# Three 256-column matmuls a block in the feature-major projections of a two-layer decoder trunk, in place of one of 512 and one of 256

## The chip, the core and the metric

The kernel runs on one core of a Trainium2 chip. The core has engines that run side by side, each with its own stream of instructions: TensorE (matmuls, in the profile PE, with its weight loads apart as PEld), VectorE (DVE), ScalarE (ACT) and GpSimd (POOL); SyncE (SP) starts most transfers here. They meet through semaphores. A matmul takes a stationary operand of 128 x 128, which a weight load brings into the array, and streams the columns of a moving operand past it; the sums go to PSUM, a memory of eight banks of 512 fp32 columns on 128 partitions. The metric is the device time of one execution, in microseconds (us).

## The reference

Two layers of a decoder trunk over 256 tokens of width 2048, in fp32. In both a normed input goes through a mixer and then through a gated MLP of hidden width 5632, each with a residual:

```python
for l in range(DEPTH):
    h = rms_norm(x, mix_norm[l])
    if l % 2 == 0:
        h = mixer_ab(h, ...)   # gMLP and HGRN2, one input and one output projection
    else:
        h = mixer_c(h, ...)    # attention with forgetting, 16 heads, output gate
    x = x + h
    h = rms_norm(x, ffn_norm[l])
    x = x + conv_ffn(h, ffn_w_up[l], ffn_conv_w[l], ffn_conv_b[l], ffn_w_down[l])
```

The gated MLP projects up to 2 x 5632 features, convolves each over three tokens, multiplies `silu(a) * b`, and projects down. Nearly all the arithmetic is in products of a 256 x 2048 (or 256 x 5632) activation with weights that are used once.

## The kernel before

**Layout.** The residual is held feature-major: `xT` is 16 tiles of 128 features x 256 tokens. `S` is 256 tokens, `P` 128.

**Precision by halves.** Operands of the big products have the type fp32r, and each fp32 value is split into a rounded part and the rest. A weight tile `w` arrives by a transfer from SyncE's queue (line 137), ScalarE makes the rounded `wh` (line 139), VectorE the rest `wl = w - wh` (line 141). An activation tile `a` of 128 x 512 holds the rounded part in columns 0 to 255 and the rest in columns 256 to 511 (`split`, lines 198 to 206). A product is then wh·ah + wh·al + wl·ah.

**Feature-major projections.** `project` (line 144) makes one tile of 128 output features x 256 tokens. It runs over blocks of 128 input features: 16 in two chunks of 8, or 11 in chunks of 6 and 5 for the down projection. For each block:

```python
PE.matmul(ps, wh[:, k * P:(k + 1) * P], a, ...)                        # 512 columns
PE.matmul(ps[:, S:2 * S], wl[:, k * P:(k + 1) * P], a[:, 0:S], ...)    # 256 columns
```

The first multiplies wh with both parts of the activation, into columns 0 to 255 and 256 to 511 of the PSUM tile; the second adds wl with the rounded part into columns 256 to 511. So at the end the two halves of the tile have to be added. `fold` (line 185) does so: ScalarE copies the second half to a tile `ev`, VectorE adds the first half to it; `project_norm` (line 191) then multiplies with the norm's factor `R` on VectorE. `add_x` (line 262) does the same for the residual: a ScalarE copy of the second half, and two VectorE additions to `xT[m]`. The projections that go this way are f, q, g and u of the first mixer (8 each) and its output (16), the forget gate, output gate and output of the second (1, 16, 16), and in each layer's gated MLP 88 for up and 64 for down.

**Token-major projections.** `project_tok` (line 162) has the activation as the stationary operand and 512 columns of weights as the moving one, three matmuls of 512 columns a block (lines 176 to 178). It serves v and i of the first mixer and q, k, v of the second.

**Order.** Work is issued in the order of the code, and the framework puts in the semaphores. Small matmuls of the mixers (tiles `px` and `pd`, in plain fp32 or fp32r) are put between the chunks of the projections by generators that `tick` advances. The PSUM pool `pm` has three tiles of one bank each, which the projections take in turn. Weights go through rings of buffers of their own (four of `w`, three or two of `wh` and `wl`).

Of the kernel before, what the change touches and what calls it, by code (L numbers as in the profile page):

```python
# [7 lines left out]
F32 = mybir.dt.float32  # L8
F32R = mybir.dt.float32r
BF16 = mybir.dt.bfloat16  # L10
AF = mybir.ActivationFunctionType
ALU = mybir.AluOpType
AX = mybir.AxisListType

P = 128
S = 256
# [28 lines left out]
def tile_trunk(ctx: ExitStack, tc: tile.TileContext, x, pp_d, cst_d, mlev_d, msk_d,  # L45
               w_v, w_f, w_g, w_i, w_q, w_u, w_abo, w_cf, w_cqkv, w_cg, w_co, w_up, w_dn, spw_d, spb_d, out):
    nc = tc.nc
    V, SC, PE = nc.vector, nc.scalar, nc.tensor
# [4 lines left out]
    tp = ctx.enter_context(tc.tile_pool(name="tp", bufs=2))  # L53
    pm = ctx.enter_context(tc.tile_pool(name="pm", bufs=3, space=bass.MemoryType.PSUM))
# [4 lines left out]
    def nm(base):  # L59
        count[0] += 1  # L60
        return f"{base}_{count[0]}"

    xT = []
    xload = []
    for c0, n in ((0, 2), (2, 2), (4, 4), (8, 4), (12, 4)):
        t = cp.tile([P, n, S], F32, tag=f"x{c0}", name=f"x{c0}")
# [31 lines left out]
    def back(ap):  # L98
        return view(ap, P - 1, (-1, P))

    def bank(tag="px"):
        n = nm(tag)
        return px.tile([P, 512], F32, tag=tag, name=n, bufs=banks[tag])
# [4 lines left out]
    def tick():  # L108
        while queue and len(flight) < depth[0]:
            flight.append(queue.pop(0))  # L110
        for g in list(flight):
            if next(g, flight) is flight:
                flight.remove(g)
# [16 lines left out]
    def weights(src, n):  # L130
        deep["turn"] += 1
        if deep["pool"] is not None and deep["turn"] > 6 and deep["turn"] % 2:
            pool, nw, ns = deep["pool"], 4, 2
        else:
            pool, nw, ns = wp, 4, 3
        w = pool.tile([P, n], F32, tag="w", name=nm("w"), bufs=nw)
        nc.sync.dma_start(w, src)
        wh = pool.tile([P, n], F32R, tag="wh", name=nm("wh"), bufs=ns)
        SC.activation(wh, w, AF.Copy)  # L139
        wl = pool.tile([P, n], F32R, tag="wl", name=nm("wl"), bufs=ns)  # L140
        V.tensor_tensor(wl, w, wh.bitcast(F32), ALU.subtract)  # L141
        return wh, wl

    def project(wsrc, acts, chunks=(8, 8), k0=0):
        ps = pm.tile([P, 512], F32, tag="pm", name=nm("pm"))
        nk = sum(chunks)
        done = 0
        for c in chunks:
            lo = (k0 + done) * P
            tick()  # L150
            wh, wl = weights(wsrc[:, lo:lo + c * P], c * P)
            for k in range(c):
                a = acts[done + k]
                first, last = done + k == 0, done + k == nk - 1
                PE.matmul(ps, wh[:, k * P:(k + 1) * P], a,  # L155
                          start=first, stop=False, skip_group_check=True)
                PE.matmul(ps[:, S:2 * S], wl[:, k * P:(k + 1) * P], a[:, 0:S],  # L157
                          start=False, stop=last, skip_group_check=True)
            done += c
        return ps  # L160

    def project_tok(wsrc, norm, feed=False):
        ps = [pm.tile([P, 512], F32, tag="pm", name=nm("pm")) for _ in range(2)]
        k = 0
        for c in ((1, 1, 1, 1) + (2,) * 6 if feed else (2,) * 8):
            if feed:
                for i in range(c):
                    norm.feed_split(k + i)
            tick()
            wh, wl = weights(wsrc[:, k * 512:(k + c) * 512], c * 512)  # L170
            for T in range(2):
                for i in range(c):
                    a = norm.a[k + i]
                    ah, al = a[:, T * P:(T + 1) * P], a[:, S + T * P:S + (T + 1) * P]
                    h, l = (t[:, i * 512:(i + 1) * 512] for t in (wh, wl))
                    PE.matmul(ps[T], ah, h, start=k + i == 0, stop=False)  # L176
                    PE.matmul(ps[T], ah, l, start=False, stop=False)  # L177
                    PE.matmul(ps[T], al, h, start=False, stop=k + i == KT - 1)  # L178
            if feed:
                for i in range(c):  # L180
                    norm.feed_square(k + i, nc.gpsimd)
            k += c
        return ps

    def fold(ps):
        t = tp.tile([P, S], F32, tag="ev", name=nm("ev"), bufs=3)
        SC.activation(t, ps[:, S:2 * S], AF.Copy)  # L187
        V.tensor_tensor(t, ps[:, 0:S], t, ALU.add)  # L188
        return t

    def project_norm(wsrc, acts, R, out=None):
        t = fold(project(wsrc, acts))
        if out is None:
            out = t
        V.tensor_tensor(out, t, R, ALU.mult)  # L195
        return out

    def split(dst, src, gain=None):
# [61 lines left out]
            return R, Rt  # L260

    def add_x(m, ps):
        t = tp.tile([P, S], F32, tag="ev", name=nm("ev"), bufs=3)
        SC.activation(t, ps[:, S:2 * S], AF.Copy)
        V.tensor_tensor(xT[m], xT[m], ps[:, 0:S], ALU.add)
        V.tensor_tensor(xT[m], xT[m], t, ALU.add)

# [1 line left out]
    def mixer_ab(norm):  # L269
        es = ExitStack()  # L270
        hp = es.enter_context(tc.tile_pool(name="hp", bufs=1))
# [4 lines left out]
        def keep(n):  # L276
            return hp.tile([P, S], F32, tag="keep", name=nm(n), bufs=3 * NH)

        # gMLP's v, two groups of four heads with the tokens on the partitions
        gv, late = [], []  # L280

        def finish():
# [6 lines left out]
        for g in range(2):  # L289
            ps = project_tok(w_v[g], norm, feed=g == 0)  # L290
            v = hp.tile([P, 2, 512], F32, tag="tok", name=nm("gv"), bufs=2)
# [5 lines left out]
            else:  # L297
                drain()
                R, Rt = late
                for T in range(2):  # L300
                    act(v[:, T], ps[T], AF.Gelu, scale=Rt[:, T:T + 1])
        A = norm.a
# [50 lines left out]

        queue.append(mixes())

        # the lower bound, softmax over the first axis of gamma
        gam = pp[:, C_GAM:C_GAM + 3 * NH]
        gm = hp.tile([P, 4 * NH], F32, tag="gm", name="gm")
        mx, sm_, lb, omlb = (gm[:, i * NH:(i + 1) * NH] for i in range(4))
# [16 lines left out]
        for h in range(NH):  # L376
            z = project_norm(w_f[h], A, R)
            l = keep("lf")
            t = hp.tile([P, 2, S], F32, tag="two", name=nm("kq"), bufs=2 * NH)
            act(l[:, 0:P], z[:, 0:P], AF.Sigmoid)  # L380
            act(back(l[:, P:S]), z[:, P:S], AF.Sigmoid)
            act(t[:, 0], z, AF.Sigmoid, scale=-1.0)
            V.tensor_scalar(t[:, 1, P:S], back(t[:, 0, P:S]), omlb[:, h:h + 1], None, ALU.mult)
            V.tensor_scalar(t[:, 0, 0:P], t[:, 0, 0:P], omlb[:, h:h + 1], None, ALU.mult)
            lf.append(l)
            kq.append(t)
# [92 lines left out]
                                       ALU.mult, ALU.mult)  # L479

        for h in range(NH):
            z = fold(project(w_q[h], A))
            V.tensor_tensor(kq[h][:, 1, 0:P], z[:, 0:P], R[:, 0:P], ALU.mult)
            V.tensor_tensor(back(kq[h][:, 0, P:S]), z[:, P:S], R[:, P:S], ALU.mult)
            queue.append(hgrn(h))
            if h % 4 == 0:
                ps = project_tok(w_i[h // 4], norm)
                itok = hp.tile([P, 2, 512], F32, tag="tok", name=nm("itok"), bufs=2)
                for T in range(2):
                    SC.activation(itok[:, T], ps[T], AF.Copy, scale=Rt[:, T:T + 1])  # L490
                ps = bank()
                PE.matmul(ps, cst[:, K_REV:K_REV + P], itok[:, 1], start=True, stop=True)
                SC.activation(itok[:, 1], ps, AF.Copy)
                itoks.append(itok)
            sg.append(project_norm(w_g[h], A, R, keep("sg")))
# [16 lines left out]
        for h in range(NH):  # L512
            z = hp.tile([P, S], F32, tag="zu", name=nm("zu"), bufs=5)
# [16 lines left out]
        for m in range(KT):  # L530
            add_x(m, project(w_abo[m], ks))
            nxt.feed(m)
        es.close()
        return nxt

# [1 line left out]
    def mixer_c(norm):  # L537
        es = ExitStack()
        hp = es.enter_context(tc.tile_pool(name="cpool", bufs=1))
# [109 lines left out]
        for m in range(KT):  # L649
            add_x(m, project(w_co[m], yB))  # L650
            nxt.feed(m)
        es.close()
        return nxt

# [1 line left out]
    def ffn(l, norm, last):  # L656
        es = ExitStack()
        hp = es.enter_context(tc.tile_pool(name="fp", bufs=1))
# [32 lines left out]
        def down(g, hid):  # L691
            for m in range(KT):
                add_x(m, project(w_dn[l, m], hid, chunks=(6, 5), k0=g * GRP))
                if g == HT // GRP - 1:
                    if last:
                        nc.sync.dma_start(out[:, m, :], xT[m])
                    else:
                        nxt.feed(m)
# [9 lines left out]

    banks.update(px=3, pd=2)
    norm = mixer_ab(Norm(C_MIX))  # L710
    norm = ffn(0, norm, False)
    norm = mixer_c(norm)
# [81 lines left out]
```

## Time and profile before

| | |
|---|---|
| median of 3 runs | 2390.4 us (2376.39, 2390.4, 2390.91) |
| span of the profiled execution | 2389.0 us, 1.4 us under the median |
| matmuls and weight loads | 13198 and 13198 |
| busy: TensorE, weight loads, VectorE, ScalarE | 2377.3, 2060.0, 1756.3, 1317.2 us |
| moved by DMA | 440.73 MB, 184 GB/s on average |

The span runs from the first to the last instruction of the profiled execution; its whole time is a little longer, and is taken to be the median. In the rows of the profile stand the line of the kernel, the engine, the operation, the tile written and those read, the count, the busy time and the mean duration in ns, and then the idle time of the engine before these instructions with what ended it. Ends of matmuls are modelled, and successive matmuls overlap in the records, so distances between starts say more than durations.

### The profile page before, as it was taken

The page shows a single profiled execution, that of the slowest core. Times are in us where ns is not written, and L with a number is a line of the kernel's source. Part 1 is how long each engine was busy: PE and PEld are TensorE (multiplying, and loading weights), DVE is VectorE, ACT ScalarE, POOL GpSimd, SP SyncE. Part 2 cuts the span into 40 slices and gives each one's busy share as a digit, 9 for nine tenths or more (in the row PEclk, how much of TensorE's full clock was granted, in tenths as well). Part 3 has the DMA queues.
Part 4 walks back from the last instruction along what each step waited for, and adds up shares of the span by engine and source line. Part 5 has one row for each costly group of instructions (what it writes and reads, how often), then busy time and mean ns, then how long its engine had stood idle before and what let it go on. Part 6 is the DMA issues. An engine that isn't in the chain of part 4 may idle for free.

```text
span 2389.0 us, 35728 instructions
## 1 busy us (share of the span) xinstructions
PE 2377.3 (100%) x13198; PEld 2060.0 (86%) x13198; DVE 1756.3 (74%) x2954; ACT 1317.2 (55%) x2169; POOL 16.1 (1%) x20
## 2 busy tenths in 40 slices
PE   8999999999999999999999999999999999999999
PEld 7888888888888888888888888888888888888888
DVE  6767786888867877777756666777777767767765
ACT  6655565655555555555545455556555555545543
POOL 2000000000000000000000000000000000000000
PEclk9999999999999999999999999999999999999999
DMA  7544455755566566566655555557555565565564
GB/s 265 177 159 135 141 184 187 241 190 191 169 187 213 177 173 222 176 170 188 200 175 177 175 159 167 188 192 237 186 186 186 156 220 186 152 220 185 153 188 145
DMA packets 133869, 440.73 MB, mean 184 GB/s; under 512 B 14880, under 2 KB 16944, under 8 KB 133440
## 3 DMA queue, kind: packets, MB, share of 16 engines
q1 hardware_dynamic: 132224, 433.40, 57.5%
q10 hardware_dynamic: 1440, 5.01, 0.6%
q8 instruction: 104, 1.70, 0.3%
q14 instruction: 69, 0.57, 0.1%
q0 software_dynamic: 32, 0.05, 0.0%
HBM read 436.29 MB, written 2.11 MB: 184 GB/s over the span
## 4 chain that ended last, share of the span: by engine, by line
PE 97%; DMA 1%; DVE 1%; issue 0%; ACT 0%; SPq 0%; DVEq 0%; ACTq 0%
PE pm L155 53%; PE pm L157 27%; PE pm L177 5%; PE pm L178 5%; PE pm L176 5%; PE px L439 1%; DVE wl L141 0%; DMA w<-in_w_v 0%; DMA mst<-in_mlev 0%; PE pd L411 0%; DMA w<-in_w_up 0%; PE pd L412 0%; PE px L612 0%; PE px L576 0%; PE px L583 0%
## 5 line engine op out<-in xcount | busy, mean ns | idle before, releaser
L141 DVE TENSOR_TENSOR wl<-w,wh 128x1024 fp32r<-128x1024 f32 (+3 forms) x900 | 1015.7, 1129 | 538.1 <-ACT wh L139 534.3
L139 ACT ACTIVATE wh<-w 128x1024 fp32r<-128x1024 f32 (+3 forms) x900 | 883.4, 982 | 952.2 <-PE pm L155 653.4
L155 PE MATMUL pm<-a,wh 128*128 128x512 f32 x3600 | 1266.0, 396 | 0.0
L157 PE MATMUL pm<-a,wl 128*128 128x256 f32 x3600 | 1010.5, 281 | 0.5 <-DVE wl L141 0.5
L155 PEld LDWEIGHTS pm<-a,wh 128*128 128x128 f32 x3600 | 675.0, 187 | 157.1 <-DVE a L204 0.8
L157 PEld LDWEIGHTS pm<-a,wl 128*128 128x128 f32 x3600 | 680.3, 189 | 1.6 <-DVE wl L141 0.8
L155 PE MATMUL pm<-hid,wh 128*128 128x512 f32 x1408 | 493.1, 395 | 0.0
L157 PE MATMUL pm<-hid,wl 128*128 128x256 f32 x1408 | 394.8, 280 | 0.0
L155 PEld LDWEIGHTS pm<-hid,wh 128*128 128x128 f32 x1408 | 263.9, 187 | 61.9
L157 PEld LDWEIGHTS pm<-hid,wl 128*128 128x128 f32 x1408 | 266.0, 189 | 0.0
L176 PE MATMUL pm<-wh,a 128*128 128x512 f32 x512 | 204.0, 400 | 2.1 <-ACT wh L139 2.1
L177 PE MATMUL pm<-wl,a 128*128 128x512 f32 x512 | 202.0, 395 | 3.5 <-DVE wl L141 3.5
L178 PE MATMUL pm<-wh,a 128*128 128x512 f32 x512 | 201.6, 394 | 0.0
L177 PEld LDWEIGHTS pm<-wl,a 128*128 128x128 f32 x512 | 97.0, 189 | 25.3 <-DVE wl L141 5.9
L176 PEld LDWEIGHTS pm<-wh,a 128*128 128x128 f32 x512 | 97.2, 190 | 21.7 <-ACT wh L139 2.4
L178 PEld LDWEIGHTS pm<-wh,a 128*128 128x128 f32 x512 | 96.7, 189 | 20.2
L673 ACT ACTIVATE conv<-ev,pp 128x256 f32<-128x256 f32 x176 | 103.4, 587 | 16.2 <-DVE ev L195 16.2
L188 DVE TENSOR_TENSOR ev<-pm,ev 128x256 f32<-128x256 f32 x225 | 93.8, 417 | 3.4 <-ACT ev L187 3.4
L674 DVE SCALAR_TENSOR_TENSOR conv<-ev,pp,conv 128x255 f32<-128x255 f32 x176 | 84.2, 478 | 8.1 <-ACT conv L673 8.1
L675 DVE SCALAR_TENSOR_TENSOR conv<-ev,pp,conv 128x254 f32<-128x254 f32 x176 | 85.1, 483 | 6.2
L155 PE MATMUL pm<-yc,wh 128*128 128x512 f32 x256 | 88.8, 391 | 0.0
L195 DVE TENSOR_TENSOR ev<-ev,R 128x256 f32<-128x256 f32 x184 | 78.3, 425 | 6.1
(181 smaller groups left out, 1602.7 us busy)
## 6 DMA issues: line engine op xcount, KB each, us to landing
w<-in_w_up SPq DMA_DIRECT2D x352, 512.0 KB, 4.3
w<-in_w_dn SPq DMA_DIRECT2D x128, 384.0 KB, 3.2
w<-in_w_cqkv SPq DMA_DIRECT2D x96, 512.0 KB, 3.6
w<-in_w_dn SPq DMA_DIRECT2D x128, 320.0 KB, 3.3
w<-in_w_abo SPq DMA_DIRECT2D x32, 512.0 KB, 4.3
w<-in_w_cg SPq DMA_DIRECT2D x32, 512.0 KB, 3.9
w<-in_w_co SPq DMA_DIRECT2D x32, 512.0 KB, 3.5
w<-in_w_f SPq DMA_DIRECT2D x16, 512.0 KB, 3.6
```

The source lines that it names most:

```text
L139: SC.activation(wh, w, AF.Copy)
L141: V.tensor_tensor(wl, w, wh.bitcast(F32), ALU.subtract)
L155: PE.matmul(ps, wh[:, k * P:(k + 1) * P], a, start=first, stop=False, skip_group_check=True)
L157: PE.matmul(ps[:, S:2 * S], wl[:, k * P:(k + 1) * P], a[:, 0:S], start=False, stop=last, skip_group_check=True)
L176: PE.matmul(ps[T], ah, h, start=k + i == 0, stop=False)
L177: PE.matmul(ps[T], ah, l, start=False, stop=False)
L178: PE.matmul(ps[T], al, h, start=False, stop=k + i == KT - 1)
L188: V.tensor_tensor(t, ps[:, 0:S], t, ALU.add)
L195: V.tensor_tensor(out, t, R, ALU.mult)
L673: SC.activation(c, z, AF.Identity, bias=pp[:, cb:cb + 1], scale=w(2))
L674: V.scalar_tensor_tensor(c[:, 1:], z[:, :S - 1], w(1), c[:, 1:], ALU.mult, ALU.add)
L675: V.scalar_tensor_tensor(c[:, 2:], z[:, :S - 2], w(0), c[:, 2:], ALU.mult, ALU.add)
```

## The change

Each block is computed by three matmuls of 256 columns, all into the same 256 columns of PSUM: wh with the rounded part, wh with the rest, wl with the rounded part. The PSUM tile still takes a bank, of which half is used. There are no halves left to add: `fold` is gone, `project_norm` and the q projection multiply straight out of PSUM, and `add_x` is a single addition. Some comment lines are emptied too, and the lines after 190 move up.

```diff
     def project(wsrc, acts, chunks=(8, 8), k0=0):
-        ps = pm.tile([P, 512], F32, tag="pm", name=nm("pm"))
+        ps = pm.tile([P, 512], F32, tag="pm", name=nm("pm"))[:, 0:S]
...
-                PE.matmul(ps, wh[:, k * P:(k + 1) * P], a,
-                          start=first, stop=False, skip_group_check=True)
-                PE.matmul(ps[:, S:2 * S], wl[:, k * P:(k + 1) * P], a[:, 0:S],
-                          start=False, stop=last, skip_group_check=True)
+                h, l = (t[:, k * P:(k + 1) * P] for t in (wh, wl))
+                PE.matmul(ps, h, a[:, 0:S], start=first, stop=False)
+                PE.matmul(ps, h, a[:, S:2 * S], start=False, stop=False)
+                PE.matmul(ps, l, a[:, 0:S], start=False, stop=last)
...
-    def fold(ps):
-        t = tp.tile([P, S], F32, tag="ev", name=nm("ev"), bufs=3)
-        SC.activation(t, ps[:, S:2 * S], AF.Copy)
-        V.tensor_tensor(t, ps[:, 0:S], t, ALU.add)
-        return t
-
     def project_norm(wsrc, acts, R, out=None):
-        t = fold(project(wsrc, acts))
+        ps = project(wsrc, acts)
         if out is None:
-            out = t
-        V.tensor_tensor(out, t, R, ALU.mult)
+            out = tp.tile([P, S], F32, tag="ev", name=nm("ev"), bufs=3)
+        V.tensor_tensor(out, ps, R, ALU.mult)
         return out
...
     def add_x(m, ps):
-        t = tp.tile([P, S], F32, tag="ev", name=nm("ev"), bufs=3)
-        SC.activation(t, ps[:, S:2 * S], AF.Copy)
-        V.tensor_tensor(xT[m], xT[m], ps[:, 0:S], ALU.add)
-        V.tensor_tensor(xT[m], xT[m], t, ALU.add)
+        V.tensor_tensor(xT[m], xT[m], ps, ALU.add)
...
-            z = fold(project(w_q[h], A))
+            z = project(w_q[h], A)
```

## The prediction

> **What bounds the kernel now.** I read the page from the top: engines, slices, chain, groups.
>
> ```profile
> span 2389.0 us, 35728 instructions
> PE 2377.3 (100%) x13198; PEld 2060.0 (86%) x13198; DVE 1756.3 (74%) x2954; ACT 1317.2 (55%) x2169; POOL 16.1 (1%) x20
> PEclk9999999999999999999999999999999999999999
> PE 97%; DMA 1%; DVE 1%; issue 0%; ACT 0%; SPq 0%; DVEq 0%; ACTq 0%
> PE pm L155 53%; PE pm L157 27%; PE pm L177 5%; PE pm L178 5%; PE pm L176 5%; PE px L439 1%; DVE wl L141 0%; DMA w<-in_w_v 0%; DMA mst<-in_mlev 0%; PE pd L411 0%; DMA w<-in_w_up 0%; PE pd L412 0%; PE px L612 0%; PE px L576 0%; PE px L583 0%
> L155 PE MATMUL pm<-a,wh 128*128 128x512 f32 x3600 | 1266.0, 396 | 0.0
> L157 PE MATMUL pm<-a,wl 128*128 128x256 f32 x3600 | 1010.5, 281 | 0.5 <-DVE wl L141 0.5
> ```
>
> TensorE is the bound: it waits 11.7 us (2389.0 − 2377.3) in all, its clock is full, and the chain lies on it for 97%. The pair of lines 155 and 157 alone is 80% of the chain. The waits on weights stand in the last column and are half a microsecond over the whole run. So the question is only how long TensorE takes for a block, and the means of 396 and 281 ns can't say it: they overlap, since ends are modelled. What counts is the distance from start to start. I count starts in long stretches: line 155's matmuls in 600 us of each layer's gated MLP, where nearly nothing but such pairs runs.
>
> ```profile
> core 0: us, PE busy (x) PEld busy (x), PEclk, DMA share, GB/s
> 500.00:1100.00 600.00, 600.00 (x1732) 323.68 (x1731) 1.00 0.61 187
> 1700.00:2300.00 600.00, 600.00 (x1699) 319.05 (x1698) 1.00 0.58 183
> ```
>
> A pair takes 600/1732 = 346.4 ns in layer 0 and 600/1699 = 353.1 ns in layer 1, with the same code and the same clock. The kernel has 5520 pairs: 257 projections of 16 blocks (32 in the first mixer and 16 for its output, 17 and 16 in the second, two times 88 for up) and 128 of 11 for down. I take 350 ns as their mean; 5520 × 0.350 = 1932 us, which is 81% of the span, as the chain has it. How these 350 ns divide between a matmul's columns and the matmul itself, with its weight load, decides the case.
>
> The token-major projections have only 512-column matmuls. Starts on TensorE, in two stretches; the middle number is the modelled duration:
>
> ```profile
> start us, us, engine line op out<-in xcount [idle before <-releaser]
> 1179.63 0.39 PE L177 MATMUL pm<-wl,a 128*128 128x512 f32 x1
> ...
> 1181.21 0.39 PE L178 MATMUL pm<-wh,a 128*128 128x512 f32 x1
> ...
> 999.88 0.28 PE L157 MATMUL pm<-a,wl 128*128 128x256 f32 x1
> 999.99 0.39 PE L155 MATMUL pm<-a,wh 128*128 128x512 f32 x1
> 1000.22 0.28 PE L157 MATMUL pm<-a,wl 128*128 128x256 f32 x1
> 1000.34 0.39 PE L155 MATMUL pm<-a,wh 128*128 128x512 f32 x1
> 1000.57 0.28 PE L157 MATMUL pm<-a,wl 128*128 128x256 f32 x1
> 1000.68 0.39 PE L155 MATMUL pm<-a,wh 128*128 128x512 f32 x1
> 1000.91 0.28 PE L157 MATMUL pm<-a,wl 128*128 128x256 f32 x1
> 1001.03 0.39 PE L155 MATMUL pm<-a,wh 128*128 128x512 f32 x1
> ```
>
> Token-major, seven matmuls from 1179.63 to 1181.21: 226 ns for 512 columns (1.58 / 7). In the pair, from a 256-column start to the next start 0.11, 0.12, 0.11 and 0.12 us; I take 117 ns, in the upper half of what the rounding leaves. The 512-column matmul then has 346.4 − 117 = 229 ns to its successor.
>
> **The change part by part.** *Matmuls.* Per block one of 512 and one of 256 columns become three of 256. The columns stay 768. Matmuls and, as every matmul in this trace has its own (13198 and 13198), weight loads go from two to three: 5520 more of each. The wh block is loaded twice in a row; nothing in the trace shows a load left out.
>
> Three readings of the rows price a matmul of 256 columns:
> (a) *The remainder.* Take the 226 ns of a 512-column matmul from the pair of layer 0: 346.4 − 226 = 120.4 ns, and three are 361 ns. In numbers for columns and matmuls that is (226 − 120.4)/256 = 0.41 ns a column and 120.4 − 256 × 0.4125 = 15 ns a matmul.
> (b) *The direct distance.* The 256-column matmul stands 117 ns from its successor, with a whole weight load beside it, as each of the three would have. Three are 350 ns.
> (c) *Columns alone.* Half of 226 is 113, which the shortest distances of 0.11 touch; three are 339 ns.
> I take (a), because (b) has to explain why the 512 columns of a pair then take 229 where the same shape takes 226 in the token-major rows, and (c) why the pair isn't 339. Stamps of the two shapes can be shifted by a few ns against one another, but the sum of a pair can't. 361 − 350 = 11 ns on 5520 blocks: **+61 us**.
>
> The bounds: (c) gives −11 ns, −61 us. Upwards, layer 1's rhythm: 353.1 less 768 × 0.4125 = 317 leaves 36 for two matmuls, 18 each, so 3 × (106 + 18) = 371 ns, +116 us. It isn't a matter of the place in the program; the rhythm sets in within one stretch of the same blocks, some us after layer 1's gated MLP began:
>
> ```profile
> 1637.36 0.39 PE L155 MATMUL pm<-a,wh 128*128 128x512 f32 x1
> ...
> 1642.22 0.39 PE L155 MATMUL pm<-a,wh 128*128 128x512 f32 x1
> ...
> 1643.03 0.70 PE L249 MATMUL px<-acc,ones 128*128 128x256 f32 x2
> ...
> 1644.04 0.40 PE L155 MATMUL pm<-a,wh 128*128 128x512 f32 x1
> ...
> 1651.09 0.40 PE L155 MATMUL pm<-a,wh 128*128 128x512 f32 x1
> ```
>
> Fourteen pairs from 1637.36 to 1642.22, 347 ns each; then the norm's two matmuls and a short disturbance; and 20 pairs from 1644.04 to 1651.09, 352.5 each. So a rhythm can change by the phase in which the engine resumes, and which one the three equal matmuls take can't be read here.
>
> The Trainium skill has a rule for this, in "TensorE: Matmul & The Clock Gate", section Back-to-back issue gap: columns over 2.4 plus 2.5 ns. By it the pair would be 325 ns and the three 327.5, and the change would cost 2.5 ns a block, an estimate of 14 us. The trace doesn't agree: 346 to 353 for the pair.
>
> *Weight loads.* Could the loads, now three in 350 ns, become the bound? Loads on TensorE where short matmuls of another kind stand between pairs:
>
> ```profile
> 73.61 0.52 PEld L338 LDWEIGHTS px<-wt,gv 128*128 128x128 f32 x4
> 74.06 0.19 PEld L155 LDWEIGHTS pm<-a,wh 128*128 128x128 f32 x1
> 74.17 0.19 PEld L157 LDWEIGHTS pm<-a,wl 128*128 128x128 f32 x1
> ```
>
> Four loads in 0.52 us of which the last takes 0.19: 0.11 us from one to the next, and 0.11 from 74.06 to 74.17. So a load can follow a load by 0.11 us; beside 117 or 120 ns there is room, but less than 10 ns, where today every second load has the 0.23 us of the long matmul. If the slack is too small, the time of a matmul with a load in its shadow is the remainder of the slow rhythm: 353.1 − 226 = 127, three are 381 ns, +171 us. The outer end, loads that don't overlap at all at 0.19 us each, would be 570 ns; the 0.11 above excludes it.
>
> *Issue.* TensorE's instructions, matmul and load, go from 4 in 346.4 ns (87 each) to 6 in 361 (60 each). The nearest rows:
>
> ```profile
> 172.03 0.94 PE L439 MATMUL px<-E 128*128 128x128 f32 x7
> 172.81 0.39 PE L443 MATMUL px<-E 128*128 128x128 f32 x2
> 173.03 0.83 PE L439 MATMUL px<-E 128*128 128x128 f32 x6
> 173.70 0.27 PE L398 MATMUL px<-cst,lf 128*128 128x128 f32 x1
> ```
>
> Fifteen matmuls with their loads from 172.03 to 173.70: 111 ns, so 56 ns an instruction, enough; but for 30 instructions, which could have been queued. I take no cost, and keep the doubt for the range. The Trainium skill, "TensorE: Matmul & The Clock Gate", section "Wait — 56ns, not 53.3ns?", has a figure of about 62 ns per matmul where a sequencer's microcode decodes; if loads cost the same, the six would take 372 ns a block, an estimate of +121 us. No run here shows which decoding is on.
>
> *Folding.* Gone are 385 ScalarE copies and 385 VectorE operations (one of each in 225 folds, and in 160 residual additions):
>
> ```profile
> L187 ACT ACTIVATE ev<-pm x225: 360/366/384, 68.7 to 2261.0; 128x256 f32<-128x256 f32 x113
> L188 DVE TENSOR_TENSOR ev<-pm,ev x225: 403/417/425, 70.0 to 2261.9; 128x256 f32<-128x256 f32 x113
> L264 ACT ACTIVATE ev<-pm x160: 358/366/385, 340.8 to 2384.9; 128x256 f32<-128x256 f32 x160
> L266 DVE TENSOR_TENSOR x<-x,ev x160: 424/425/428, 342.5 to 2385.8; 128x256 f32<-128x256 f32 x160
> ```
>
> 141 us of ScalarE (385 × 0.366) and 162 us of VectorE (225 × 0.417 + 160 × 0.425). All of it but the last steps lies beside TensorE's work; both engines feed the weights (lines 139 and 141), for which TensorE hardly waits, so it buys next to nothing. Uncovered is the end: the copy at 2384.93, the last addition from 2385.80 for 0.42. With one addition in place of the three steps the last output leaves some 0.9 us sooner. The same chain stands at the three other stage borders, where of the 11.7 us of waiting about 1 us can be it. I take **−2 us**. The accumulator needs half a bank but still takes a whole one of three; it is freed sooner, for which nobody waits. No queue's transfers move: the loads of weights are paced by TensorE.
>
> Sum: 2389.0 + 61 − 2 = 2448 us of span; the median of the runs is 2390.4, so 1.4 us lie around it: **2449 us**, 2.5% more. Of the runs 2376.39 is 14 us below the two others; the 2112 blocks of layer 1's gated MLP (88 × 16 + 64 × 11) at 6.7 ns less are 14.2 us, so that run may have held layer 0's rhythm throughout. A change of under 1% (24 us) can't be told from none in this kernel.
>
> **The rivals.**
> 1. *A 256-column matmul stays at its direct distance*, reading (b): 350 ns a block, 0 − 2 us, **2388 us**, not slower. For it: the distances shown, none over 0.12. Against it: the remainder to the 226 of the long matmul. It decides the case if the distance after a 256-column matmul stays at or below 117 with a load behind every one; at 120 the forecast holds. The Trainium skill's rule above, a small sum per instruction, would end here too.
> 2. *A faster rhythm.* Equal matmuls and loads may fall into step at (c)'s 113, 339 ns: 2389.0 − 61 − 2 + 1.4 = **2327 us**, faster than before. It decides where the load's 0.11 us just fits beside the columns. For it: two rhythms of one code exist, and the 0.11. Against it: no stretch holds it.
> 3. *Loads or issue bound*: 371 to 381 ns, **2504 to 2559 us**. For it: the small slack of the loads, and no long run at this rate. Against it: 0.11 us for load after load and 56 ns an instruction.
> 4. *The second load of wh is left out*, so that the change adds no load: two loads as before, so 350 ns if (a)'s 15 ns hang on the loads: the time of rival 1, and counted there. Against it: equal counts of loads and matmuls.
>
> **How the numbers follow.** The forecast has 0.46 (its own range 2420 to 2504, from a stretch-wise mix with 350 to the 371 ns of the slow rhythm), rival 1 with 4 has 0.26, rival 2 0.12, rival 3 0.16. The range 2370 to 2515 holds the forecast, rival 1 (within 18 us) and the lower half of rival 3; it leaves out 0.12 below and 0.08 above. Faster by over 1% is rival 2 and a little of rival 1, 0.13; within 1% the rest of rival 1 and the forecast's lowest edge, 0.27; slower 0.60.
>
> **What the profile after would show.** 18718 matmuls and as many loads (13198 + 5520); in 600 us of the gated MLP about 4990 starts of the block's matmuls if the forecast holds (600 / 0.1204), 5140 with rival 1, 5310 with rival 2, 4720 to 4850 with rival 3, where loads would lie 0.12 to 0.13 apart without a gap. ScalarE loses about 141 us of busy time and VectorE 162; the last output's chain has one VectorE step. TensorE still has 97% of the chain. Wrong would prove the forecast a distance of 117 or less over long stretches, or a wait of TensorE on anything but itself.

## The result, and the profile after

The changed kernel takes 2445.0 us (median of 4 runs, 2444.5 to 2445.1) against 2390.7 us: a ratio of 1.0235, 95% interval 1.021 to 1.0259. The forecast was 2449. The times of the kernel before lie on three levels, near 2377, 2391 and 2406 us, and those of the changed kernel within 0.6 us of each other; the last section has what is known of the levels.

The page of the changed kernel, its header, engines, clock, the chain by engine, and its costliest groups on TensorE:

```profile
span 2442.7 us, 45994 instructions
PE 2431.5 (100%) x18718; PEld 2357.9 (97%) x18718; DVE 1628.9 (67%) x2569; ACT 1211.0 (50%) x1784; POOL 16.3 (1%) x20
PEclk9999999999999999999999999999999999999999
...
PE 97%; DVE 1%; DMA 1%; issue 0%; ACT 0%; SPq 0%; DVEq 0%; ACTq 0%
...
L156 PE MATMUL pm<-a,wh 128*128 128x256 f32 x3600 | 1022.5, 284 | 0.0
L157 PE MATMUL pm<-a,wh 128*128 128x256 f32 x3600 | 1020.3, 283 | 0.0
L158 PE MATMUL pm<-a,wl 128*128 128x256 f32 x3600 | 1019.5, 283 | 0.5 <-DVE wl L141 0.5
```

TensorE is still all of the chain; its waits are 11.2 us (2442.7 − 2431.5), where they were 11.7. Matmuls and loads have grown by 5520 each. So the 53.7 us between the two spans are TensorE's own pace. Starts are counted in the same stretches of the gated MLPs; the numbers in brackets behind PE are matmuls of all three lines together:

```profile
core 0: us, PE busy (x) PEld busy (x) DVE busy (x) ACT busy (x) POOL busy (x), PEclk, DMA share, GB/s
500.00:1100.00 600.00, 600.00 (x5003) 600.00 (x5002) 404.29 (x584) 288.12 (x390) 0.00 (x0) 1.00 0.61 180
1700.00:2300.00 600.00, 600.00 (x5002) 600.00 (x5001) 409.69 (x589) 290.78 (x394) 0.00 (x0) 1.00 0.61 183
```

600/5003 is 119.9 ns from one matmul to the next, 359.8 a block, and now the same in both layers. Against the mean of 350 before that is 9.8 ns on 5520 blocks, 54 us. The weight loads are busy for the whole stretch. In the order of time, TensorE's starts and the loads' beside them:

```profile
2000.04 0.28 PE L158 MATMUL pm<-a,wl 128*128 128x256 f32 x1
2000.16 0.28 PE L156 MATMUL pm<-a,wh 128*128 128x256 f32 x1
2000.28 0.28 PE L157 MATMUL pm<-a,wh 128*128 128x256 f32 x1
2000.40 0.28 PE L158 MATMUL pm<-a,wl 128*128 128x256 f32 x1
```

```profile
2000.04 0.19 PEld L156 LDWEIGHTS pm<-a,wh 128*128 128x128 f32 x1
2000.16 0.19 PEld L157 LDWEIGHTS pm<-a,wh 128*128 128x128 f32 x1
2000.28 0.19 PEld L158 LDWEIGHTS pm<-a,wl 128*128 128x128 f32 x1
```

Every 0.12 us a matmul starts, and with it the load for the next one; the wh block is indeed loaded twice. The end of the chain is shorter, as the rows of the last output show, first in the kernel before, then in the changed one:

```profile
2384.57 0.28 PE L157 MATMUL pm<-hid,wl 128*128 128x256 f32 x1
2385.80 0.42 DVE L266 TENSOR_TENSOR x<-x,ev 128x256 f32<-128x256 f32 x1
```

```profile
2439.24 0.28 PE L158 MATMUL pm<-hid,wl 128*128 128x256 f32 x1
2439.55 0.42 DVE L257 TENSOR_TENSOR x<-x,pm 128x256 f32<-128x256 f32 x1 [3.54 <-PE pm L158]
2440.00 0.33 SPq L687 DMA_DIRECT2D out<-x  x1
```

From the last matmul's start to the end of the span it is 2442.7 − 2439.24 = 3.5 us, where it was 2389.0 − 2384.57 = 4.4.

### The profile page after: what moved, and what is told of

Same layout as the page of the kernel before. It is cut to its first block, busy times and chain, and to the rows that moved or that the text cites. A ratio compares the mean times of both kernels' runs of the same rounds, so it can differ in the third digit from the quotient of the medians.

```text
span 2442.7 us, 45994 instructions
## 1 busy us (share of the span) xinstructions
PE 2431.5 (100%) x18718; PEld 2357.9 (97%) x18718; DVE 1628.9 (67%) x2569; ACT 1211.0 (50%) x1784; POOL 16.3 (1%) x20
## 4 chain that ended last, share of the span: by engine, by line
PE 97%; DVE 1%; DMA 1%; issue 0%; ACT 0%; SPq 0%; DVEq 0%; ACTq 0%
PE pm L157 27%; PE pm L158 27%; PE pm L156 27%; PE pm L177 4%; PE pm L178 4%; PE pm L176 4%; DVE wl L141 1%; PE px L430 1%; DMA w<-in_w_v 0%; DMA mst<-in_mlev 0%; PE pd L403 0%; PE pd L402 0%; PE px L567 0%; PE px L574 0%; PE px L603 0%
## 5 line engine op out<-in xcount | busy, mean ns | idle before, releaser
L156 PE MATMUL pm<-a,wh 128*128 128x256 f32 x3600 | 1022.5, 284 | 0.0
L157 PE MATMUL pm<-a,wh 128*128 128x256 f32 x3600 | 1020.3, 283 | 0.0
L158 PEld LDWEIGHTS pm<-a,wl 128*128 128x128 f32 x3600 | 690.8, 192 | 1.0 <-DVE wl L141 0.7
L157 PEld LDWEIGHTS pm<-a,wh 128*128 128x128 f32 x3600 | 691.0, 192 | 0.7 <-issue 0.2
L156 PEld LDWEIGHTS pm<-a,wh 128*128 128x128 f32 x3600 | 690.9, 192 | 0.4
L157 PE MATMUL pm<-hid,wh 128*128 128x256 f32 x1408 | 398.7, 283 | 0.0
L156 PE MATMUL pm<-hid,wh 128*128 128x256 f32 x1408 | 398.7, 283 | 0.0
L156 PEld LDWEIGHTS pm<-hid,wh 128*128 128x128 f32 x1408 | 270.4, 192 | 0.0
L157 PEld LDWEIGHTS pm<-hid,wh 128*128 128x128 f32 x1408 | 270.4, 192 | 0.0
L189 DVE TENSOR_TENSOR ev<-pm,R 128x256 f32<-128x256 f32 x184 | 78.0, 424 | 94.8 <-PE pm L158 94.5
```

The costliest lines, as they stand in the source:

```text
L156: PE.matmul(ps, h, a[:, 0:S], start=first, stop=False)
L157: PE.matmul(ps, h, a[:, S:2 * S], start=False, stop=False)
L158: PE.matmul(ps, l, a[:, 0:S], start=False, stop=last)
L189: V.tensor_tensor(out, ps, R, ALU.mult)
```

## The experiments

The theory to test: a matmul with its load costs 120 ns at 256 columns, by columns and a fixed part, and the folds were hidden. What is the fixed part: the number of matmuls, the load's length, the type of the operands? Where only a span is given, the kernel ran once. In the code, `h` and `l` are the block's parts of wh and wl, and `...` marks what is left out.

**The matmuls without the folds' change.** The kernel before with three matmuls a block, but into two halves, with all folds.

```diff
-                PE.matmul(ps, wh[:, k * P:(k + 1) * P], a, ...)
-                PE.matmul(ps[:, S:2 * S], wl[:, k * P:(k + 1) * P], a[:, 0:S], ...)
+                PE.matmul(ps[:, 0:S], h, a[:, 0:S], ...)
+                PE.matmul(ps[:, S:2 * S], h, a[:, S:2 * S], ...)
+                PE.matmul(ps[:, S:2 * S], l, a[:, 0:S], ...)
```

> The kernel before with three 256-column matmuls a block, but into the two halves as before, and with all folds kept; the result is whole. Theory (a matmul with its load costs 120 ns whatever columns of PSUM it writes, folds are hidden): 360 ns a block, a span of 2443 to 2446 us, 2.3% over the kernel before. Rival (the loss comes from adding three times into the same 256 columns, or from evicting straight out of PSUM): 350 ns a block and about 2390 us.

Measured: 2447.6 us, ratio 1.0243 (1.0188 to 1.0298), a span of 2446.3. Its windows:

```profile
500.00:1100.00 600.00, 600.00 (x5003) 1.00 0.61 180
1700.00:2300.00 600.00, 600.00 (x5002) 1.00 0.62 183
```

The very counts of the changed kernel. So the loss is the third matmul with its load; where it adds and how it is evicted doesn't change the pace. The folds are worth 3.6 us by the spans (2446.3 − 2442.7), 2.6 by the medians; TensorE's idle time is 13.5 us with them (2446.3 − 2432.8) and 11.2 without. These are two separate sets of runs, and within one level the times of the kernel before scatter by 3 us, so the size is rough.

**The folds' change without the matmuls.** The changed kernel with the pair of 512 and 256 columns put back, and the short evictions kept: the second half of the tile is not added.

```diff
-        return ps
+        return ps[:, 0:S]
```

> The matmuls of the kernel before (512 and 256 columns), evicted as after the change: no folds, one addition to the residual. The second half is not added, so two of the three products are left out of the result; TensorE's work is that of before. Theory: the folds were hidden, a span 1 to 3 us below the kernel before in the same rhythm (2386 to 2388 us, or 2373 to 2375 where layer 1 runs at 346.7 ns a block). Rival (the shorter evictions cost or gain more than the last steps): over 10 us away from both.

Measured: 2378.5 us (10 runs from 2377.2 to 2407.0), ratio 0.9977 (0.9937 to 1.0016). The profiled execution, with a span of 2375.9 us, has the fast rhythm in both layers, as the starts of line 155 show, at 346.6 ns a block (600/1731):

```profile
500.00:1100.00 600.00, 600.00 (x1732) 323.70 (x1731) 1.00 0.61 187
1700.00:2300.00 600.00, 600.00 (x1731) 323.62 (x1732) 1.00 0.61 187
```

The times lie on the levels of the kernel before, whose 13 runs beside them lay between 2376.6 and 2407.2; a gain of 1 to 3 us can't be told among them. It excludes the rival's 10 us.

**272 columns.** The changed kernel with 16 more columns in each matmul, which don't belong to the product.

```diff
-                PE.matmul(ps, h, a[:, 0:S], start=first, stop=False)
-                PE.matmul(ps, h, a[:, S:2 * S], start=False, stop=False)
-                PE.matmul(ps, l, a[:, 0:S], start=False, stop=last)
+                PE.matmul(ps, h, a[:, 0:272], start=first, stop=False)
+                PE.matmul(ps, h, a[:, 240:512], start=False, stop=False)
+                PE.matmul(ps, l, a[:, 0:272], start=False, stop=last)
```

> The changed kernel with 272 columns in each of the three matmuls; the result is spoilt by 16 columns that don't belong. Theory (columns plus a fixed part a matmul): 16 x 0.41 = 6.7 ns more for each, 126.7 ns from start to start, 380 ns a block, a span of 2553 us. Rival (the 120 ns are the floor of the weight load, and the matmul itself takes 113 to 117): 120 to 124 ns, 360 to 371 a block, 2443 to 2503 us.

Measured: a span of 2519.7 us.

```profile
500.00:1100.00 600.00, 600.00 (x4824) 1.00 0.59 174
1700.00:2300.00 600.00, 599.92 (x4819) 1.00 0.61 182
```

124.4 ns a matmul (600/4824): 4.5 more than at 256 columns, not 6.7. That is between the two, just above the rival's end of 124, and alone it decides nothing. It does say that the straight line through 256 and 512 isn't exact in between.

**A third matmul of 128 columns.** The changed kernel, with the product of wl left out for half of the tokens.

```diff
-                PE.matmul(ps, l, a[:, 0:S], start=False, stop=last)
+                PE.matmul(ps[:, 0:P], l, a[:, 0:P], start=False, stop=last)
```

> The changed kernel with 128 columns in the third matmul of a block: the product of wl is left out for half the tokens. Theory with no floor: 120 + 120 + 68 = 308 ns a block, 2155 us. Theory with the load's floor of 111 ns a load: 3 loads make 333 at least, and the short matmul 111 instead of 68: 351 ns, 2393 us. Rival (the load's floor is the 120 itself): 360 ns, 2443 us. Time over 2443 us would say that fewer than 256 columns of this type run slower, which no row shows.

Measured: a span of 2391.0 us, 600 / (5161/3) = 348.8 ns a block. Its windows, and the starts of its loads:

```profile
500.00:1100.00 600.00, 600.00 (x5161) 1.00 0.63 186
```

```profile
1999.83 0.19 PEld L158 LDWEIGHTS pm<-a,wl 128*128 128x128 f32 x1
1999.95 0.19 PEld L156 LDWEIGHTS pm<-a,wh 128*128 128x128 f32 x1
2000.06 0.19 PEld L157 LDWEIGHTS pm<-a,wh 128*128 128x128 f32 x1
2000.17 0.19 PEld L158 LDWEIGHTS pm<-a,wl 128*128 128x128 f32 x1
2000.29 0.19 PEld L156 LDWEIGHTS pm<-a,wh 128*128 128x128 f32 x1
2000.40 0.19 PEld L157 LDWEIGHTS pm<-a,wh 128*128 128x128 f32 x1
```

Halving the columns of one matmul in three saves 11 ns a block, not 52, as the middle expectation had it. The load of line 156 starts with the short matmul of line 158, and the next load follows it after 0.11 us both times: the load is the floor of a short matmul. Since that floor is 0.11, it alone isn't what makes a 256-column matmul take 0.12.

**Two of 384 columns.** The changed kernel with the same 768 columns in two matmuls; part of the products is left out or put in wrong columns.

```diff
+                PE.matmul(ps, h, a[:, 0:384], start=first, stop=False)
+                PE.matmul(ps, l, a[:, 0:384], start=False, stop=last)
```

> The changed kernel with two matmuls of 384 columns a block in place of three of 256 (the same 768 columns; part of the products is left out or put in wrong columns). Theory (0.4125 ns a column and 15 ns a matmul with its load): 2 x 173.4 = 347 ns a block in both layers, a span of 2370 us. Rival (columns alone): 339 ns and 2327 us. Rival (the slow rhythm is a matter of two loads a block): 353 ns in some stretches, up to 2405 us.

Measured: a span of 2372.7 us.

```profile
500.00:1100.00 600.00, 600.00 (x3463) 1.00 0.61 187
1700.00:2200.00 500.00, 500.00 (x2887) 1.00 0.61 190
```

173.3 and 173.2 ns a matmul, 346.5 a block in both MLPs: the pair's time in its fast rhythm. With the same 768 columns, two matmuls cost the same whether they are 512 + 256 or 384 + 384, and a third costs 13 ns. So it is the number of matmuls with their loads. From 256 to 384 columns a matmul grows by 173.3 − 119.9 = 53.4 ns, 0.417 ns a column; the columns are then 107 ns of the 120, and the fixed part is 13.

Not every stretch of this kernel has that pace. In the output of the first mixer two starts of line 156 that lie 195 blocks apart are these, 353.3 ns a block:

```profile
345.19 0.34 PE L156 MATMUL pm<-yb,wh 128*128 128x384 f32 x1
414.09 0.34 PE L156 MATMUL pm<-yb,wh 128*128 128x384 f32 x1
```

That is the pair's slow rhythm with two equal matmuls, as the last rival of the expectation had it, though in a short stretch and in neither MLP.

**Shorter loads.** The changed kernel, with 64 or with 32 stationary columns in the second and third matmul of a block. These matmuls then also write 64 or 32 partitions of PSUM, so the load isn't all that shrinks.

```diff
-                PE.matmul(ps, h, a[:, S:2 * S], start=False, stop=False)
-                PE.matmul(ps, l, a[:, 0:S], start=False, stop=last)
+                PE.matmul(ps[0:64], h[:, 0:64], a[:, S:2 * S], ...)
+                PE.matmul(ps[0:64], l[:, 0:64], a[:, 0:S], ...)
```

> The changed kernel with only 64 of the 128 stationary columns in the second and third matmul of a block, so that two of three loads are half as long; the moving columns stay 256 (two products are left out for half of the output features). Theory (the 13 ns above 107 come from the load that runs beside the stream): the first and second matmul, beside which the short loads run, come down by half of it to about 113 ns, the third stays at 120: 347 ns a block, a span of 2443 - 73 = 2370 us. Rival (a fixed part of an fp32r matmul, whatever is loaded): 360 ns, 2443 us.

> The same with 32 stationary columns. Theory: a quarter of the 13 ns, 110 + 110 + 120 = 340 ns a block, 2332 us. Rival (fixed part): 360 ns, 2443 us.

Measured: spans of 2388.0 and 2389.3 us. For 32 columns, the loads by line and the window of layer 0; below them, for 64 columns, the gate and output projections of the second mixer:

```profile
L156 PEld LDWEIGHTS pm<-a,wh 128*128 128x128 f32 x3600 | 675.8, 188 | 31.8
L157 PEld LDWEIGHTS pm<-a,wh 128*32 128x32 f32 x3600 | 388.7, 108 | 0.7 <-issue 0.2
L158 PEld LDWEIGHTS pm<-a,wl 128*32 128x32 f32 x3600 | 386.8, 107 | 33.2 <-DVE wl L141 1.3 <-issue 0.3
```

```profile
500.00:1100.00 600.00, 600.00 (x5145) 1.00 0.63 185
```

```profile
1498.00:1636.00 138.00, 138.00 (x1196) 1.00 0.65 191
```

The loads do get shorter (188 to 108 ns), but a block takes 349.9 ns (1800/5145) with 32 columns and, with 5146 matmuls, the same with 64. Both expectations were wrong. In the MLPs a shorter load gives back 10 ns of a block, 3.3 a matmul, and half the length gives as much as a quarter; by the stamps, the matmul beside the one long load comes down with the others, to 117 or 118 ns. The other 10 ns a matmul above the columns' 107 stay. But with 64 columns a block of the second mixer takes 346.2 ns (138 / (1196/3)), so the pace changes from stretch to stretch here too, and 350 can't be read as the price of the loads alone.

**The type.** The split operands in bf16 in place of fp32r, in the kernel before (the pair) and in the changed one (the three); the products are coarser, and what that does to accuracy was not studied.

```diff
-        wh = pool.tile([P, n], F32R, tag="wh", name=nm("wh"), bufs=ns)
+        wh = pool.tile([P, n], BF16, tag="wh", name=nm("wh"), bufs=ns)
```

(and likewise for wl and every activation tile).

> The kernel before with the split operands in bf16 in place of fp32r (both parts, weights and activations; the result is coarser), so that a weight load reads half the bytes. Theory (the 15 ns a matmul come from the load's reading beside the stream): they fall away mostly, about 325 ns a block and 213 to 216 for the 512-column matmuls of the token-major part, a span of 2235 to 2260 us. Rival (they belong to any matmul): 347 to 353 ns, 2375 to 2390 us.

> The changed kernel with the split operands in bf16 likewise. Theory (the third load costs because of its reading): the three matmuls cost hardly more than the pair, 325 to 335 ns a block, 2240 to 2300 us, and the difference to the bf16 pair is under 20 us. Rival (a fixed part for any matmul): 53 us over the bf16 pair, as with fp32r.

> The bf16 pair again, timed for an interval: 2245 us, 0.94 of the kernel before; 325 ns a block in both layers, and all runs within 2 us of each other, if without the long loads there are no rhythms. Rival (the rhythms belong to the unequal pair): runs 14 and 28 us apart, as before.

Measured: the pair a span of 2243.7 us, the three 2254.2. Timed again, the pair took 2245.5 us, ratio 0.9347 (0.9308 to 0.9385), with all four runs between 2244.8 and 2246.8. The seven runs of the kernel before beside it lay on its two upper levels (2390.7 to 2409.0); against 2377 the ratio would be 0.945. The pair's windows and its loads, then the window of the three:

```profile
500.00:1100.00 600.00, 599.97 (x3693) 1.00 0.65 198
1700.00:2200.00 500.00, 500.00 (x3079) 1.00 0.66 199
```

```profile
L155 PEld LDWEIGHTS <-wh 128*128 128x128 bf16 x5520 | 540.5, 98 | 647.5 <-issue 3.4
```

```profile
500.00:1100.00 600.00, 600.00 (x5499) 1.00 0.67 197
```

A bf16 pair takes 324.9 ns (1200/3693) and in layer 1 324.8 (1000/3079), the three 327.3 (1800/5499). The pair is as unequal as before and keeps one pace, so unequal matmuls alone don't make the rhythms. The third matmul costs 2.4 ns in bf16 where it costs 13 in fp32r, and the difference of the kernels is 10.5 us, not 54: 2.4 × 5520 = 13 less the 3 that the folds give. By the Trainium skill's formula in "TensorE: Matmul & The Clock Gate", section Back-to-back issue gap, which the page gives for an isolated matmul, the estimates are 325 and 327.5 ns. The trace agrees for bf16, 324.9 and 327.3, and not for fp32r, 346.5 to 353.3 and 359.8.

**The rhythms.** The kernel before, with a small matmul ahead of every eighth up projection.

```diff
+            if j % 8 == 0:
+                nudge = bank()
+                PE.matmul(nudge[:, 0:P], ones, ones, start=True, stop=True)
             z = project_norm(w_up[l, j], A, R)
```

> The kernel before with one 128-column fp32 matmul on constants put ahead of every eighth up projection in both layers (22 in all, nobody reads them). Theory (two rhythms, and the phase in which TensorE resumes picks one): both 346.7 and 353.3 ns a block are found in both layers, changing only at such a matmul or a wait; the span moves by up to 14 us either way. Rival (the rhythm belongs to the layer): 346.7 throughout layer 0 and 353.3 throughout layer 1.

Measured: a span of 2397.6 us. Starts of line 155 in four stretches, two in each layer's MLP:

```profile
566.00:652.00 86.00, 85.91 (x249) 46.38 (x248) 1.00 0.56 180
850.00:1140.00 290.00, 289.81 (x821) 154.07 (x820) 1.00 0.63 184
1985.00:2068.00 83.00, 82.91 (x240) 44.72 (x239) 1.00 0.56 178
2075.00:2380.00 305.00, 304.81 (x863) 161.97 (x862) 1.00 0.62 184
```

Layer 0 has 346 and 353 ns a block, and layer 1 too (86/249, 290/821, 83/240, 305/863, each to within one start). In the MLPs' up projections the pace changed only at such a matmul. The rhythm isn't the layer's.

## Why the prediction was right

- *What bounds.* Right: TensorE, with 11 us of waits before and after, and all of the difference in its own pace.
- *The price of the third matmul.* Reading (a), the remainder of 120.4 ns, against 119.9 measured. The pair's sum gave it and the stamps inside the pair didn't: the direct distance of 117 would have been 350 ns a block, and rival 1 with it. For the span the forecast had 61 − 2 = 59 us, and the spans show 53.7. Rounded rows made the remainder 0.5 ns too high, 120.4 for 119.9, and that times three on 5520 blocks is 8 us; some 3 us the other way were not traced. It also matters from which level one counts: the 54 us are the distance from the middle one of the three.
- *The straight line* of 0.41 ns a column and 15 ns a matmul is right at 256 and 384 columns (120 and 173; the 226 at 512 went into it), 2 to 3 ns too high at 272, and wrong at 128, where the load's 0.11 us is the floor. Its 15 ns come out as 13.
- *The upper bound from the slow rhythm*, 371 ns, didn't occur: the three equal matmuls showed no second pace in either MLP.
- *Rival 1* didn't occur. The prediction lets the Trainium skill's rule end at this rival too; by its own estimate of 14 us for that rule the time would be near 2402 us, between the rival's 2388 and the forecast.
- *Rival 2* (113 ns) didn't occur. *Rival 3*: the loads are at 0.12 us without a gap, as it said, but they follow the matmuls; their own floor of 0.11 was shown, and the issue of six instructions in 327 ns in the bf16 run excludes issue as the bound at 360. *Rival 4* didn't: every matmul has its load.
- *The folds.* −2 us were forecast; the two kernels with three matmuls show 2.6 to 3.6, of which 0.9 is the end. 385 operations went on each engine, and no wait of TensorE in the profile before was put down to one of them. The page's busy times fall by only 106 and 127 us, where 141 and 162 were forecast from the durations: busy time counts overlapping records once, and the count times the mean was the wrong way to forecast it. Added up record by record, the durations fall by 144 and 161 us.

## What to carry to other kernels

Where matmuls of two shapes alternate, take the price of a shape from sums over long stretches and from a stretch of one shape alone, not from the start stamps inside a pair. In fp32r, each matmul with its own weight load cost some 13 ns beyond its columns, so that one matmul over 512 columns beat two over 256, though it needs a fold; the folds cost some 3 us here, where the other engines had room. Before trimming instructions at such a bound, look at the operand type: in bf16 the same part was 2.4 ns, and the kernel 5.5 to 6.5% faster by the level that one counts from, where the coarser products can be borne.

## What the runs showed that was not expected

- *Several rhythms of one instruction stream.* In the gated MLPs, pairs of 512 and 256 fp32r columns run at 346.5 or at 353.3 ns a block, at full clock, and change only where something else comes between. The 6.8 ns on the 2112 blocks of an MLP are 14 us, and the runs of the kernel before lie near 2377, 2391 and 2406 us: that none, one or both MLPs were slow fits these steps. Profiled runs show two of the three cases, one slow MLP in the kernel before (2389.0 us) and none in the run without folds (2375.9); both slow was not profiled. By the stamps of the trace the slow rhythm's extra lies behind the 512-column matmul, 236 ns on average in place of 230, while the 256-column one stays at 117. In the output of the first mixer the kernel before has a third pace, 199 blocks between these two starts, 350.0 ns each:

```profile
345.01 0.39 PE L155 MATMUL pm<-yb,wh 128*128 128x512 f32 x1
414.66 0.39 PE L155 MATMUL pm<-ya,wh 128*128 128x512 f32 x1
```

Two of 384 columns show 353.3 in the same place, as said above. The three of 256 with full loads and the bf16 kernels kept one pace in every long stretch. What makes a rhythm is open. Against its own fast rhythm the change costs 68 us (2445 − 2377), not 54.
- *The fixed part is not the load's length.* Of the 13 ns a matmul, 3 went in the MLPs when two loads of three were halved, no more when they were quartered, and 11 went with bf16, which changes the stream and the load at once. The rhythms, of up to 7 ns a block, blur the first two numbers. Whether the rest lies in reading fp32r columns or in switching weights stays open; no matmul without a load, and none of mixed type, was tried.
